# A hybrid two-layer backbone on one core: the last modulation chunks quarter by quarter, group 0 normed ahead, the pooling mean by a constant, the first mixer weights fetched sooner

## The chip, the core and the metric

The kernel runs on one core of a Trainium2 chip. The core has five engines that work side by side: TensorE (PE: matmuls; its weight loads are listed apart as PEld), VectorE (DVE), ScalarE (ACT), GpSimd (POOL) and SyncE (SP), which here only issues DMAs from HBM. The metric is the device time of one launch, in microseconds (us); lower is better. The time before is 3062.89 us, the median of 3 runs.

## What is computed

Two streams, latent `x` (256 tokens of width 2048) and context `ctx` (256 tokens), pass through two layers. Each layer has a token mixer and a gated MLP, both behind an RMS norm with a shift, a scale and a gate that come from the conditioning vectors through `w_mod`. Layer 0's mixer is a centred mean over 2, 4, 8 or 16 tokens (one window for each quarter of the channels) minus the token itself, then a 512x512 matrix for each channel group:

```python
POOL_WINDOWS = (2, 4, 8, 16)

def pool_mix(u, w, b, scale):
    for g, win in enumerate(POOL_WINDOWS):
        left, right = win // 2, win - 1 - win // 2
        ug = uf[..., g * POOL_GROUP:(g + 1) * POOL_GROUP]
        cs = jnp.cumsum(jnp.pad(ug, ((0, 0), (left + 1, right), (0, 0))), axis=1)
        window_sum = cs[:, win:win + T] - cs[:, :T]
        count = (jnp.minimum(t + right, T - 1) - jnp.maximum(t - left, 0) + 1).astype(jnp.float32)
        parts.append(window_sum / count[None, :, None] - ug)
    y = jnp.einsum('btgc,gcd->btgd', p, w).reshape(B, T, D) + b
    return y * scale

for i in range(DEPTH):                       # DEPTH = 2
    ml = (silu_c @ w_mod[i] + b_mod[i]).reshape(B, 6, 1, D)
    a_lat = modulate(rms_norm(h, norm1_g[i]), ml[:, 0], ml[:, 1])
    h = h + ml[:, 2] * mixer(a_lat)          # pool_mix in layer 0, attention in layer 1
    h = h + ml[:, 5] * conv_ffn(modulate(rms_norm(h, norm2_g[i]), ml[:, 3], ml[:, 4]), ...)
```

`count` is the window's width but for the first and last few tokens, where the window is cut off. The change concerns layer 0 alone: its modulation, its mixer and the start of its MLP.

## The kernel before

The hidden state is held transposed, as 16 tiles of 128 channels by 256 tokens for each stream (`hl`, `hc`). Every large product is made in float32 precision by three matmuls: weights and activations are split into a high part (`h`, made by ACT) and the rest (`l`, made by DVE) in a reduced type, and hi·hi, hi·lo and lo·hi are summed.

**Modulation.** Layer 0's modulation has 24 chunks of 512 outputs; chunk `4*w+g` belongs to use `w` (0 shift, 1 scale, 2 gate of the mixer; 3 to 5 the same of the MLP) and channel group `g`. `mod_pe` (L195) makes one chunk on PE: four quarters `g` of the contraction, each fetched as two DMAs of 512 KB into two tiles, in order. Two quarters are multiplied together: sixteen matmuls (L207), the first of which waits for the four DMAs of both. Then ACT copies the sum out of PSUM (`modev`, L219), PE transposes it (`modt`, L224) and DVE makes `modT` from it. The generator `mods` (L440) goes through the chunks in the order 0, 4, 8, 16, 12, then the same plus 1 and so on for each channel group, and 20 to 23 (the MLP's gate) last. `need(n)` (L453) advances it until n quarters have been issued.

**Rooms.** A fetched tile takes a staging room: six rooms of their own (`NW`), and such activation buffers (`A4` to `A15`) as are not yet in use, which `lend` adds and takes away by group and step (`LENT`, L41). `stage` (L115) hands the rooms out strictly in turn, so a DMA waits until the tile that was in its room half a ring or more before has been used. From step 13 of the last group on only the six rooms are left, three pairs.

**The mixer** (`mixer`, L461) is a generator too, one for each channel group: for its four channel tiles, DVE multiplies h by the scale and the norm's factor (`py`, L474), ACT adds the shift into a padded tile (`pad`, L476), DVE sums the window by doubling (`ws`, L482), POOL multiplies by a table of 1/count (`pf`, L487), DVE subtracts the token (L488) and splits (`ph`). After the fourth, the mixer's weights `wp` are loaded and split (L494). Then PE's `pm` (L505 to L507), ACT's `pz` with scale and bias, POOL's sum into the hidden state, and `Ad`, the split operand of the next products.

**The first MLP columns** (`partial`, L531) are made while the mixer works: for the first eight column tiles of the gate and up weights (`wcg`, `wcu`), the products of channel group g are made while group g+1 is mixed (`cg`, `cu`, L566 to L568, with the shift's share `pwg`, `pwu` from L549 transposed by `ptg`, `ptu`). Between them, `between(half)` (L606) calls `need`, the next step of the mixer, and in the last group the second norm, its operands (`normalise`, L373 ff.) and the gates of finished columns (`gate0`, `late`). When the last group is through, the dense stage starts with column 8 (`g`, L653). The numbers in `STEPS` (L459) say how many quarters must have been issued before each step of the first group's mixer.

**What sets the order.** The program is written in this order, but each engine's own order is then made by a scheduler from a model of the time; what an engine executes is shown by the rows further below. SP issues the DMAs in one queue, in its own order: a DMA that waits for its room holds up all behind it.

## Time and profile before

| | |
|---|---|
| median of 3 runs (lowest, highest) | 3062.89 us (3062.56, 3066.64) |
| the profiled execution's own time | 3060.9 us |
| its span in the trace | 3059.1 us |
| mean clock granted to PE | 0.989 |
| PE busy | 2977.4 us, 97% of the span |
| DVE, ACT, POOL busy | 1939.4, 1371.3, 829.1 us |
| HBM read | 554.93 MB |

The profile is of one execution. "Busy" is the time in which an engine had an instruction at work; a wait is put down to what ended last before the instruction could start. A row of a group reads: line, engine, operation, tile written <- tiles read, shape, count, then busy us and mean ns of one, then the engine's idle time just before and what ended it. A row of a window reads: stretch, length, then busy time and count for PE, PEld, DVE, ACT and POOL, the clock granted to PE (1.00 is full speed), the share of the DMA engines in use, and GB/s. A row of the chain of waits reads: start, duration, engine and what it did (DMA: from issue to landing).

### The profile page before, as it was taken

What the parts mean: (1) busy time and instruction counts of PE and PEld (TensorE: products, weight loads), DVE (VectorE), ACT (ScalarE), POOL (GpSimd) and SP (SyncE); (2) the same over time, 40 slices, a digit from 0 to 9 for tenths busy, and PEclk for the clock granted to TensorE, in tenths of its full rate; (3) what the DMA queues carried; (4) which work ended last, traced back from release to release, by engine and by line L of the source; (5) the groups of instructions that cost most, each with busy time, mean ns of one, the idle gap of its engine ahead of it and who ended that gap; (6) DMA issues with size and microseconds to landing.
All of it is one profiled execution on the core that took longest, in us unless ns stands there. A gap on an engine that the chain in (4) does not pass through costs nothing.

```text
span 3059.1 us, 40876 instructions
## 1 busy us (share of the span) xinstructions
PE 2977.4 (97%) x15082; PEld 2416.9 (79%) x15082; DVE 1939.4 (63%) x2748; ACT 1371.3 (45%) x2219; POOL 829.1 (27%) x823
## 2 busy tenths in 40 slices
PE   5999989999999999999999999999999999999998
PEld 2666668888888888888887888878888888888887
DVE  4455764386584857758586656474767666666666
ACT  3433455323333242433334444343545666666665
POOL 2111313303122030321312000000003566566665
PEclk9999989999999999999999999999999999999999
DMA  9888563384765747567482333333355555555563
GB/s 390 331 305 321 207 206 97 103 255 142 216 192 166 241 143 234 160 198 212 150 257 69 121 101 114 101 107 111 106 161 182 185 181 196 192 187 182 184 196 113
DMA packets 177927, 559.70 MB, mean 183 GB/s; under 512 B 17600, under 2 KB 22208, under 8 KB 177728
## 3 DMA queue, kind: packets, MB, share of 16 engines
q1 hardware_dynamic: 177728, 557.10, 55.7%
q8 instruction: 119, 1.95, 0.2%
q14 instruction: 80, 0.66, 0.1%
HBM read 554.93 MB, written 2.10 MB: 182 GB/s over the span
## 4 chain that ended last, share of the span: by engine, by line
PE 93%; DMA 2%; DVE 1%; POOL 1%; ACT 1%; issue 1%; SPq 0%; DVEq 0%; ACTq 0%; POOLq 0%
PE g L788 5%; PE u L788 5%; PE d L679 5%; PE d L680 5%; PE d L681 5%; PE d L835 4%; PE g L653 4%; PE g L655 4%; PE g L654 4%; PE u L655 4%; PE u L653 4%; PE u L654 4%; PE g L791 3%; PE u L791 3%; PE mod L207 2%; PE d L839 2%
## 5 line engine op out<-in xcount | busy, mean ns | idle before, releaser
L692 POOL TENSOR_TENSOR hl<-hl,dy 128x256 f32<-128x256 f32 x160 | 146.2, 914 | 941.8 <-ACT dy L691 941.6
L850 POOL TENSOR_TENSOR hl<-hl,dy 128x256 f32<-128x256 f32 x320 | 332.1, 1074 | 188.3 <-ACT dy L848 186.0
L262 DVE SCALAR_TENSOR_TENSOR macc<-wm,sc,macc 128x512 f32<-128x512 f32 (+1 forms) x360 | 328.8, 944 | 66.9 <-DMA wm<-wmod 66.2
L691 ACT ACTIVATE dy<-d,modT 128x256 f32<-128x256 f32 x320 | 133.1, 469 | 187.5 <-PE d L681 167.2
L692 POOL TENSOR_TENSOR hc<-hc,dy 128x256 f32<-128x256 f32 x160 | 129.4, 809 | 0.0
L848 ACT ACTIVATE dy<-d,modT 128x512 f32<-128x512 f32 x160 | 104.5, 684 | 43.0 <-PE d L839 41.5
L149 DVE TENSOR_TENSOR wd_2l<-wd,wd_2h 128x1024 fp32r<-128x1024 f32 (+1 forms) x44 | 54.5, 1245 | 107.8 <-ACT wd_2h L147 106.6
L207 PE MATMUL mod<-wm,sc 128*32 128x512 f32 x768 | 98.9, 641 | 15.2 <-DMA wm<-wmod 13.4
L937 POOL TENSOR_TENSOR rk<-rk,rp 128x256 f32<-128x256 f32 x16 | 13.2, 826 | 365.3 <-DVE rk L936 309.7
L149 DVE TENSOR_TENSOR wd_3l<-wd,wd_3h 128x1024 fp32r<-128x1024 f32 (+1 forms) x44 | 52.0, 1202 | 77.3 <-ACT wd_3h L147 75.9
L149 DVE TENSOR_TENSOR wd_1l<-wd,wd_1h 128x1024 fp32r<-128x1024 f32 (+1 forms) x44 | 53.7, 1224 | 54.4 <-ACT wd_1h L147 54.4
L487 POOL TENSOR_TENSOR pf<-ws,inv 128x256 f32<-128x256 f32 x32 | 29.3, 935 | 208.0 <-DVE ws L482 192.9
L149 DVE TENSOR_TENSOR wd_0l<-wd,wd_0h 128x1024 fp32r<-128x1024 f32 (+1 forms) x44 | 54.6, 1248 | 40.9 <-ACT wd_0h L147 40.9
L147 ACT CAST wd_1h<-wd 128x1024 fp32r<-128x1024 f32 (+1 forms) x44 | 45.3, 1032 | 74.8 <-PE u L654 49.4
L1026 ACT ACTIVATE sb<-sb,nm 128x512 f32<-128x512 f32 x64 | 46.1, 721 | 64.5 <-DVE nm L1022 63.3
L207 PEld LDWEIGHTS mod<-wm,sc 128*32 128x32 f32 x768 | 22.3, 114 | 65.5 <-issue 62.0
L147 ACT CAST wd_0h<-wd 128x1024 fp32r<-128x1024 f32 (+1 forms) x44 | 45.3, 1032 | 59.1 <-PE u L788 29.1
L814 DVE TENSOR_TENSOR actb<-sgb,actb 128x256 fp32r<-128x256 f32 x43 | 52.7, 1226 | 26.5 <-ACT actb L813 26.5
L679 PE MATMUL d<-act,wd_2h 128*128 128x512 f32 x172 | 67.1, 390 | 0.0
L681 PE MATMUL d<-act,wd_2l 128*128 128x512 f32 x172 | 66.9, 389 | 0.0
L680 PE MATMUL d<-act,wd_2h 128*128 128x512 f32 x172 | 66.9, 389 | 0.0
L679 PE MATMUL d<-act,wd_0h 128*128 128x512 f32 x172 | 66.9, 389 | 0.0
(1752 smaller groups left out, 9274.6 us busy)
## 6 DMA issues: line engine op xcount, KB each, us to landing
wm<-wmod SPq DMA_DIRECT2D x384, 512.0 KB, 6.1
wd<-wd SPq DMA_DIRECT2D x168, 512.0 KB, 4.4
wg<-wg SPq DMA_DIRECT2D x156, 512.0 KB, 4.7
wu<-wu SPq DMA_DIRECT2D x156, 512.0 KB, 4.5
wv<-wv SPq DMA_DIRECT2D x32, 512.0 KB, 3.7
wk<-wq SPq DMA_DIRECT2D x32, 512.0 KB, 4.0
wq<-wq SPq DMA_DIRECT2D x32, 512.0 KB, 3.6
wo<-wo SPq DMA_DIRECT2D x32, 512.0 KB, 4.2
```

The costliest lines, as they stand in the source:

```text
L149: eng.tensor_tensor(lo[:, :n], t[:, :n], hi[:, :n].bitcast(F32), op=ALU.subtract)
L262: nc.vector.scalar_tensor_tensor(acc[s], v, sc2[:, k, s : s + 1], acc[s], op0=ALU.mult, op1=ALU.add)
L653: nc.tensor.matmul(ps, hi[:, c : c + P], xh, start=(k == 0), stop=False)
L654: nc.tensor.matmul(ps, hi[:, c : c + P], xl, start=False, stop=False)
L655: nc.tensor.matmul(ps, lo[:, c : c + P], xh, start=False, stop=(k == KT - 1))
L679: nc.tensor.matmul(ps, hi[:, o : o + P], xh, start=(i == 0), stop=False)
L680: nc.tensor.matmul(ps, hi[:, o : o + P], xl, start=False, stop=False)
L681: nc.tensor.matmul(ps, lo[:, o : o + P], xh, start=False, stop=(i == n - 1))
L692: nc.gpsimd.tensor_tensor(h_of(s)[:, k, :], h_of(s)[:, k, :], y[:, s], op=ALU.add)
L788: nc.tensor.matmul(ps, hi[:, c : c + P], flat(B[k]), start=(k == 0), stop=False)
L791: nc.tensor.matmul(ps[:, T:], lo[:, c : c + P], B[k][:, 0], start=False, stop=(k == KT - 1))
L850: nc.gpsimd.tensor_tensor(hl[:, k, :], hl[:, k, :], y[:, q], op=ALU.add)
```

## The change

Five edits, all in layer 0:

1. `mod_pe`: for the chunks 21, 22 and 23 each quarter's eight matmuls go alone, behind its own two DMAs; the other chunks go in pairs of quarters as before.
2. Group 0's h times the norm's factor (eight 128x256 products on DVE, into two tiles `xn`) is made right after the norm, ahead of the modulation. When the scale and shift are there, one ACT instruction applies both and writes `pad`. Groups 1 to 3 keep `py`.
3. Pooling: the multiplication by 1/count on POOL is gone. DVE makes window sum times 1/win minus the token in one instruction. The first win/2 and the last win-1-win/2 columns of the window sum are multiplied beforehand, in place, by win/count: one tiny DVE instruction for each channel tile in group 0, two in the others.
4. `wp0` is loaded ahead of chunk 8's weights, and split where it was.
5. The last two steps of group 0's mixer ask for 15 quarters, not 17.

```diff
--- before.py
+++ after.py
@@ -195,25 +195,25 @@
     def mod_pe(l, ch, sc, pool):
 
         ps = bank("m", f"mod{l}_{ch}")
+        held = []
         for g in range(4):
             ts = load(lambda a, b: wmod[l, ch, g, :, a:b], 2048, f"wm{l}_{ch}_{g}")
-            if g % 2 == 0:
-                held, first = ts, fetched[-2:]
-            else:
-                landing = first + fetched[-2:]
+            held.append((g, ts, fetched[-2:]))
+            if ch > 20 or g % 2:
                 with ExitStack() as behind:
-                    for n, (gg, tt) in enumerate(((g, ts), (g - 1, held))):
+                    for n, (gg, tt, _) in enumerate(held[::-1]):
                         for j in (2, 3, 0, 1):
                             ins = nc.tensor.matmul(ps[32 * j : 32 * j + 32, :], sc[:, 4 * gg + j, :],
                                                    tt[j // 2][0][:, 512 * (j % 2) : 512 * (j % 2) + 512],
-                                                   start=(g == 1 and n == 0), stop=(g == 3 and n == 1),
-                                                   tile_position=(0, 32 * j))
+                                                   start=(g < 2 and (n == 0 and held[0][0] == 0)),
+                                                   stop=(g == 3 and gg == held[0][0]), tile_position=(0, 32 * j))
                             if n == 0 and j == 2:
-                                for x in landing:
+                                for x in sum((d for _, _, d in held), []):
                                     tc.add_manual_dep(ins.ins, x.name, mybir.DependencyInfo(
                                         mybir.DependencyClass.Sync, mybir.DependencyReason.DATA), reason="whole")
                                 behind.enter_context(tc.issue_after(ins.ins))
                                 behind.enter_context(tc.high_priority())
+                held = []
             if g == 3:
                 ev = pool.tile([P, 512], F32, tag="t2", name=f"modev{l}_{ch}")
                 nc.scalar.copy(ev, ps)
@@ -425,6 +425,11 @@
                 t = st.tile([P, 2, WP], F32, bufs=1, name=f"pad{j}")
                 nc.gpsimd.memset(t, 0.0)
                 pads.append(t)
+            normed = [act_tile(f"xn{j}", F32) for j in range(2)]
+            for k in range(4):
+                for s in both:
+                    nc.vector.tensor_tensor(normed[k // 2][:, k % 2, T * s : T * s + T], h_of(s)[:, k, :],
+                                            rs1[:, T * s : T * s + T], op=ALU.mult)
             shs = []
             for j in range(2):
                 t = st.tile([P, 4, 32], F32, bufs=1, name=f"sh{j}")
@@ -457,6 +462,7 @@
 
 
             STEPS = (9, 9, 9, 9, 13, 13, 17, 17)
+            STEPS0 = (9, 9, 9, 9, 13, 13, 15, 15)
 
             def mixer(g):
 
@@ -469,11 +475,16 @@
                 for i in range(4):
                     k = 4 * g + i
                     pad = pads[k % 2]
-                    y = f0.tile([P, 2, T], F32, tag="t2", name=f"py{k}")
+                    if g:
+                        y = f0.tile([P, 2, T], F32, tag="t2", name=f"py{k}")
+                    else:
+                        y = normed[k // 2][:, k % 2].rearrange("p (s t) -> p s t", s=2)
                     for s in both:
-                        nc.vector.scalar_tensor_tensor(y[:, s], h_of(s)[:, k, :], M(0, 1, k, s), rs1[:, T * s : T * s + T],
-                                                       op0=ALU.mult, op1=ALU.mult)
-                        nc.scalar.activation(pad[:, s, PAD : PAD + T], y[:, s], AF.Identity, bias=M(0, 0, k, s))
+                        if g:
+                            nc.vector.scalar_tensor_tensor(y[:, s], h_of(s)[:, k, :], M(0, 1, k, s),
+                                                           rs1[:, T * s : T * s + T], op0=ALU.mult, op1=ALU.mult)
+                        nc.scalar.activation(pad[:, s, PAD : PAD + T], y[:, s], AF.Identity, bias=M(0, 0, k, s),
+                                             scale=1.0 if g else M(0, 1, k, s))
                     src, w = pad, 1
                     while w < win:
                         n = WP - 2 * w + 1
@@ -482,16 +493,20 @@
                         nc.vector.tensor_tensor(dst[:, :, :n], src[:, :, :n], src[:, :, w : w + n], op=ALU.add)
                         src, w = dst, 2 * w
                     o = PAD - win // 2
+                    for c, n in ((0, win // 2), (T - (win - 1 - win // 2), win - 1 - win // 2)):
+                        if n:
+                            e = src[:, :, o + c : o + c + n]
+                            nc.vector.scalar_tensor_tensor(e, e, float(win), inv_t[:, c : c + n].unsqueeze(1).broadcast_to([P, 2, n]),
+                                                           op0=ALU.mult, op1=ALU.mult)
                     pf = f0.tile([P, 2, T], F32, tag="t2", name=f"pf{k}")
-                    for s in both:
-                        nc.gpsimd.tensor_tensor(pf[:, s, :], src[:, s, o : o + T], inv_t, op=ALU.mult)
-                    nc.vector.tensor_tensor(pf, pf, pad[:, :, PAD : PAD + T], op=ALU.subtract)
+                    nc.vector.scalar_tensor_tensor(pf, src[:, :, o : o + T], 1.0 / win, pad[:, :, PAD : PAD + T],
+                                                   op0=ALU.mult, op1=ALU.subtract)
                     ph = ap0.tile([P, 2, 2, T], F32R, tag=f"A{k}", name=f"ph{k}")
                     nc.scalar.copy(ph[:, 0], pf)
                     nc.vector.tensor_tensor(ph[:, 1], pf, ph[:, 0].bitcast(F32), op=ALU.subtract)
                     pa.append(ph)
                     if i == 3:
-                        parts = ld(wp[g], f"wp{g}")
+                        parts = split(early, "wp0") if g == 0 else ld(wp[g], f"wp{g}")
                     yield
                 nc.vector.tensor_tensor(gsc, modT[0, 8 + g].rearrange("p i s -> p (i s)"), V("ps")[:, 8 * g : 8 * g + 8],
                                         op=ALU.mult)
@@ -590,7 +605,9 @@
                         nc.vector.tensor_tensor(w_, w_, t_, op=ALU.add)
             lend(range(4, KT))
             mix = mixer(0)
-            for n in STEPS:
+            need(8)
+            early = load(lambda a, b: wp[0][:, a:b], 2048, "wp0")
+            for n in STEPS0:
                 need(n + 2)
                 next(mix)
             rstd = None
```

PE has as many instructions as before. DVE's list has 28 rows more, POOL's 16 fewer.

How the rows move, at three places. **The front, 20 to 82 us.** On SP (`wm_8_q_c` is half c of quarter q of chunk 8; DMAs are issued in the order of the rows), before:

```order
L131 DMA wm_8_0_0_294<-wmod 128x1024
L131 DMA wm_8_0_1024_296<-wmod 128x1024
L465 DMA inv_314<-inv 128x256
L131 DMA wm_8_2_1024_312<-wmod 128x1024
L131 DMA wm_8_2_0_310<-wmod 128x1024
L131 DMA wm_8_1_1024_300<-wmod 128x1024
L131 DMA wm_8_1_0_298<-wmod 128x1024
L131 DMA wm_8_3_1024_388<-wmod 128x1024
L131 DMA wm_8_3_0_386<-wmod 128x1024
L131 DMA wp_1024_376<-wp 128x1024
L131 DMA wp_0_374<-wp 128x1024
```

Now:

```order
L131 DMA wp_0_294<-wp 128x1024
L131 DMA wp_1024_296<-wp 128x1024
L471 DMA inv_328<-inv 128x256
L131 DMA wm_8_1_1024_314<-wmod 128x1024
L131 DMA wm_8_1_0_312<-wmod 128x1024
L131 DMA wm_8_0_1024_310<-wmod 128x1024
L131 DMA wm_8_0_0_308<-wmod 128x1024
L131 DMA wm_8_3_1024_382<-wmod 128x1024
L131 DMA wm_8_3_0_380<-wmod 128x1024
L131 DMA wm_8_2_1024_326<-wmod 128x1024
L131 DMA wm_8_2_0_324<-wmod 128x1024
```

Both halves of `wp` moved from behind chunk 8 to ahead of it, and all of chunk 8 moved back by two DMAs. On PE there, the end of chunk 12 and the first column matmuls, before:

```order
L207 MATMUL mod_12_542<-wm_12_0_1024_545,sc 32x512 x2
L207 MATMUL mod_12_542<-wm_12_0_0_543,sc 32x512 x2
L207 MATMUL mod_12_542<-wm_12_3_1024_619,sc 32x512 x2
L207 MATMUL mod_12_542<-wm_12_3_0_617,sc 32x512 x2
L207 MATMUL mod_12_542<-wm_12_2_1024_561,sc 32x512 x2
L207 MATMUL mod_12_542<-wm_12_2_0_559,sc 32x512 x2
L566 MATMUL cg_0_595<-Ad_563,wcg_0h_587 128x512
L566 MATMUL cg_1_610<-Ad_563,wcg_0h_587 128x512
```

Now:

```order
L206 MATMUL mod_12_536<-wm_12_0_1024_539,sc 32x512 x2
L206 MATMUL mod_12_536<-wm_12_0_0_537,sc 32x512 x2
L581 MATMUL cg_0_585<-Ad_541,wcg_0h_565 128x512
L581 MATMUL cg_1_604<-Ad_541,wcg_0h_565 128x512
L206 MATMUL mod_12_536<-wm_12_3_1024_613,sc 32x512 x2
L206 MATMUL mod_12_536<-wm_12_3_0_611,sc 32x512 x2
L206 MATMUL mod_12_536<-wm_12_2_1024_594,sc 32x512 x2
L206 MATMUL mod_12_536<-wm_12_2_0_592,sc 32x512 x2
```

The first two `cg` moved between the two halves of chunk 12. **The up weights of group 0** (`wcu`) on SP, before:

```order
L131 DMA wm_1_0_1024_651<-wmod 128x1024
L131 DMA wm_1_0_0_649<-wmod 128x1024
L131 DMA wcu_0_1024_718<-wu 128x2x512
L131 DMA wcu_0_0_716<-wu 128x2x512
L131 DMA wm_1_2_1024_700<-wmod 128x1024
L131 DMA wm_1_2_0_698<-wmod 128x1024
L131 DMA wm_5_1_1024_796<-wmod 128x1024
L131 DMA wm_5_1_0_794<-wmod 128x1024
```

Now:

```order
L131 DMA wm_5_0_1024_779<-wmod 128x1024
L131 DMA wm_5_0_0_777<-wmod 128x1024
L131 DMA wm_5_3_1024_827<-wmod 128x1024
L131 DMA wm_5_3_0_825<-wmod 128x1024
L131 DMA wm_5_2_1024_816<-wmod 128x1024
L131 DMA wm_5_2_0_814<-wmod 128x1024
L131 DMA wcu_0_0_710<-wu 128x2x512
L131 DMA wcu_0_1024_712<-wu 128x2x512
```

They moved twelve rows back, behind the last quarter of chunk 5. **The tail, 380 to 429 us.** On PE around chunk 22, before:

```order
L568 MATMUL cg_5_3254<-Ad_2819,wcg_4l_3185 128x512
L207 MATMUL mod_22_3234<-wm_22_1_1024_3263,sc 32x512 x2
L207 MATMUL mod_22_3234<-wm_22_1_0_3261,sc 32x512 x2
L207 MATMUL mod_22_3234<-wm_22_0_1024_3237,sc 32x512 x2
L207 MATMUL mod_22_3234<-wm_22_0_0_3235,sc 32x512 x2
L207 MATMUL mod_22_3234<-wm_22_3_1024_3330,sc 32x512 x2
L207 MATMUL mod_22_3234<-wm_22_3_0_3328,sc 32x512 x2
L207 MATMUL mod_22_3234<-wm_22_2_1024_3306,sc 32x512 x2
L207 MATMUL mod_22_3234<-wm_22_2_0_3304,sc 32x512 x2
L224 MATMUL modt_22_3364<-ident,modev_22_3340 128x128 x4
```

Now, around its last quarter:

```order
L583 MATMUL cg_5_3252<-Ad_2813,wcg_4l_3179 128x512
L206 MATMUL mod_22_3228<-wm_22_3_1024_3328,sc 32x512 x2
L206 MATMUL mod_22_3228<-wm_22_3_0_3326,sc 32x512 x2
L583 MATMUL cg_996<-Ad_2808,wcg_4l_3183 128x512
L581 MATMUL cg_996<-Ad_2813,wcg_4h_3182 128x512
L582 MATMUL cg_996<-Ad_2813,wcg_4h_3182 128x512
L583 MATMUL cg_996<-Ad_2813,wcg_4l_3183 128x512
L581 MATMUL cu_1197<-Ad_2784,wcu_4h_3405 128x512
L582 MATMUL cu_1197<-Ad_2784,wcu_4h_3405 128x512
L581 MATMUL cu_1268<-Ad_2784,wcu_4h_3405 128x512
L582 MATMUL cu_1268<-Ad_2784,wcu_4h_3405 128x512
L224 MATMUL modt_22_3358<-ident,modev_22_3334 128x128 x4
```

The quarters moved apart; matmuls of `cg` and `cu`, which do not need them, fill the places between and the one ahead of the transposes. On DVE at the tail's end, up to `late`, which the dense stage's first gate needs, before:

```order
L149 TENSOR_TENSOR wg_8l_3606<-wg_8_0_3601,wg_8h_3605 128x1024
L334 TENSOR_SCALAR A_0_3_3441<-nrm_3442,modT_14_2136,A_0_3_3441 128x256 x2
L579 TENSOR_TENSOR part_954<-part_954,cu_5_3472 128x512
L393 TENSOR_TENSOR sg_3459<-sg_3459,part_708 128x512
L400 TENSOR_TENSOR act_3462<-sg_3459,act_3462 128x512
L226 TENSOR_REDUCE modT_23_3521<-modt_23_3516 128x8
L189 TENSOR_TENSOR modT_23_3521<-modT_23_3521,vt 128x8
L589 TENSOR_REDUCE puu_4_3541<-ptu_4_3536 128x8
L376 TENSOR_TENSOR late_0_3551<-cg_960,n2acc 128x512
L376 TENSOR_TENSOR late_1_3555<-cu_1203,n2acc 128x512
```

Now:

```order
L149 TENSOR_TENSOR wg_8l_3600<-wg_8_0_3595,wg_8h_3599 128x1024
L400 TENSOR_TENSOR act_3456<-sg_3453,act_3456 128x512
L594 TENSOR_TENSOR part_948<-part_948,cu_5_3466 128x512
L149 TENSOR_TENSOR wu_8l_3661<-wu_8_0_3656,wu_8h_3660 128x1024
L149 TENSOR_TENSOR wg_8l_3604<-wg_8_1024_3597,wg_8h_3603 128x1024
L226 TENSOR_REDUCE modT_23_3515<-modt_23_3510 128x8
L189 TENSOR_TENSOR modT_23_3515<-modT_23_3515,vt 128x8
L604 TENSOR_REDUCE puu_4_3535<-ptu_4_3530 128x8
L376 TENSOR_TENSOR late_0_3545<-cg_954,n2acc 128x512
L376 TENSOR_TENSOR late_1_3549<-cu_1197,n2acc 128x512
```

Two more splits of the dense stage's weights (`wu_8l`, the second `wg_8l`) moved ahead of `late`.

## The prediction

> **What bounds the kernel now.** I read the page's first part, then the waits of TensorE (PE), then windows, then the chain of waits inside the stretches where PE is not full.
>
> ```profile
> span 3059.1 us, 40876 instructions
> PE 2977.4 (97%) x15082; PEld 2416.9 (79%) x15082; DVE 1939.4 (63%) x2748; ACT 1371.3 (45%) x2219; POOL 829.1 (27%) x823
> ```
>
> PE idles for 3059.1 − 2977.4 = 81.7 us in all. The change leaves PE's instructions as many as they were, so it can win only from this idle time and from matmuls that ran at a reduced clock, or lose by adding to them. Where the idle time lies before 450 us, by what ended it (total, times, longest):
>
> ```profile
> PE n1s L310 <- DVE n1q L303: 21.8, 1, 21.8
> PE mod L207 <- DMA wm<-wmod: 13.4, 3, 7.9
> PE modt L224 <- ACT modev L219: 11.1, 9, 3.3
> PE pwg L549 <- DVE sh L438: 3.4, 1, 3.4
> ```
>
> The 21.8 us at the start (square sums of the inputs) are not touched. The rest falls into two stretches, which the windows show (the columns from PE on are busy time and count; near the end the granted clock, DMA share and GB/s):
>
> ```profile
> 20.00:40.00 20.00, 15.08 (x86) 6.34 (x86) 3.03 (x11) 1.75 (x3) 1.03 (x1) 1.00 1.03 419
> 40.00:60.00 20.00, 12.09 (x50) 6.02 (x51) 16.35 (x29) 8.59 (x15) 6.70 (x8) 0.68 1.03 418
> 80.00:100.00 20.00, 20.00 (x125) 13.56 (x118) 5.74 (x13) 7.84 (x15) 0.00 (x0) 1.00 1.01 382
> 380.00:400.00 20.00, 12.96 (x68) 8.99 (x64) 15.25 (x29) 11.38 (x24) 3.51 (x3) 0.89 0.69 239
> 400.00:420.00 20.00, 17.37 (x87) 9.27 (x88) 11.05 (x20) 10.33 (x18) 1.74 (x1) 0.69 0.75 244
> ```
>
> In the **front** (20 to 80 us) the DMA share is 1.03: the queue is full, and an earlier transfer there only makes another later. In the **tail** (380 to 429 us) it is 0.69: there transfers wait for room, not for bandwidth. The chain of waits in the tail:
>
> ```profile
> 391.11 1.93 PE mod L207 x16
> 393.51 7.25 DMA wm<-wmod
> 403.27 4.84 DMA wm<-wmod
> 424.24 1.92 PE mod L207 x16
> 428.15 0.61 DVE late L376
> 428.80 0.50 PE g L653
> ```
>
> The first two quarters of chunk 22 leave their four rooms only when their sixteen matmuls have run (391.11 to 393.04). The last quarter is fetched into them at 393.51 and lands 7.25 us later; PE stands still. Then the same again for chunk 23: a transfer that starts at 403.27 and takes 4.84. The first matmul of the dense stage (g of column 8) comes at 428.80; from there PE has no large hole, so I count the time by how much earlier that matmul starts.
>
> **The singles in the tail.** A chunk above 20 now goes quarter by quarter: a quarter waits for two transfers instead of four and frees two rooms at once. On PE, quarters 0 to 3 of chunk 22 now stand apart between the column matmuls of group 3, where before its second sixteen stood behind all of them. What can be won is read from this row (the tail from chunk 21's end to the first dense matmul):
>
> ```profile
> 380.35:428.80 48.45, 37.17 (x197) 22.73 (x193) 31.22 (x59) 22.91 (x44) 6.58 (x5) 0.82 0.69 232
> ```
>
> PE is idle for 48.45 − 37.17 = 11.3 us of it. And what PE did right behind its holes was slow:
>
> ```profile
> 400.89 3.64 PE L207 MATMUL mod<-wm,sc 128*32 128x512 f32 x16 [7.93 <-DMA wm<-wmod]
> 408.24 3.64 PE L207 MATMUL mod<-wm,sc 128*32 128x512 f32 x16 [0.96 <-DMA wm<-wmod]
> ```
>
> Two sixteens ran in 3.64 us where the warm one at 424.24 took 1.92, which is 3.4 us more; the small work between them at the same clock (0.50) adds about 1.3. So PE alone could end 16.0 us earlier: the upper bound. VectorE (DVE) comes next: it is busy for 31.22 us, and its idle time is mostly this:
>
> ```profile
> DVE modT L226 <- PE modt L224: 13.2, 2, 10.4
> L149 DVE TENSOR_TENSOR wcg_4l<-wcg,wcg_4h 128x1024 fp32r<-128x1024 f32 x8 | 9.4, 1221 | 6.1 <-ACT wcg_4h L147 6.1
> ```
>
> The 13.2 us go away with PE's holes; the other idle time of DVE (48.45 − 31.22 − 13.2 = 4.0) I keep. By the new order two more splits of dense weights, 1.22 us each by the row of their kind, stand on DVE ahead of `late`, whose end PE awaits. So DVE ends at 380.35 + 31.22 + 4.0 + 2.4 = 418.0 where it ended at 428.8: **−10.8 us**. I take this rather than 16.0 since DVE is the longer of the two. The lower bound is the rooms: the last fourteen pairs of transfers still pass through six rooms, three pairs at a time. If only the longest hole (7.9) is halved and the clock recovers for one of the sixteens (1.7), the gain is 5.6.
>
> **The front.** `wp0` is fetched ahead of chunk 8, group 0 is normed ahead, and its scale and shift are one ScalarE (ACT) instruction.
>
> ```profile
> 40.26 10.78 DMA wp<-wp
> 51.06 1.99 ACT L147 CAST wp0h<-wp 128x1024 fp32r<-128x1024 f32 x2 [0.90 <-DMA wp<-wp]
> 54.90 1.12 PE L224 MATMUL modt<-ident,modev 128*128 128x128 f32 x4 [3.35 <-ACT modev L219]
> 56.02 0.43 PE pm L505
> 60.72 0.38 PE pm L507
> 61.33 0.23 PE pm L506
> 76.42 0.66 PE modt L224 x4
> 77.08 3.57 PE mod L207 x32
> 80.65 0.66 PE cg L566 x2
> ```
>
> `wp0` now lands where chunk 8's first half did, and the second half of chunk 8 lands at `wp0`'s old 51.04. So PE gets the last sixteen of chunk 8 at 51.04; with 1.92 for them and ACT's copy (0.6, no longer behind the 1.99 of `wp0h`) its transposes come near 54. Thus pm starts near 55, hardly sooner than now. What changes is the clock: PE works from 51 on, with no hole of 3.35 us ahead of the transposes, so pm's first dozen matmuls go at 0.23 instead of 0.43 (the spacing from 56.02 to 60.72): 12 × 0.20 = 2.4, of which I take 2.0. And of the 32 matmuls of chunk 12 (3.57 us, all between the transposes at 76.42 and the first column matmul at 80.65) the second sixteen now stand behind the first two column matmuls, which wait for chunk 16 and not for them: of their 1.8 us I take 1.1, since the column matmuls' own operands come in time for only part of it. Against it: `wcu` of group 0 now uses the rooms of `wcg` and is issued behind chunk 5, not at 78.
>
> ```profile
> 78.10 0.89 SPq L131 DMA_DIRECT2D wcu<-wu  x2
> 91.58 1.02 PE pwg L549 x16
> 97.05 0.43 PE cu L566
> DMA to landing us min/median/max: 4.2/6.7/9.0
> ```
>
> Its rooms come free with pwg, which starts at about 91.6 − 3.1 = 88.5 and takes 1.02; 4.2 to 6.7 us to land gives 93.7 to 96.3. PE wants it at 97.05 − 1.0 − 3.1 = 93.0: late by 0.7 to 3.3; cold work behind it is short, I take 1.1. Front: −2.0 − 1.1 + 1.1 = **−2.0 us**, with bounds of −4.4 (no stall, full 2.4, 2.0 for chunk 12's half) and +1 (nothing gained, `wcu` late).
>
> **The middle: pooling off GpSimd (POOL).**
>
> ```profile
> L487 POOL TENSOR_TENSOR pf<-ws,inv 128x256 f32<-128x256 f32 x32 | 29.3, 935 | 208.0 <-DVE ws L482 192.9
> L488 DVE TENSOR_TENSOR pf<-pf,pad 128x512 f32<-128x512 f32 x16 | 11.0, 687 | 7.0 <-POOL pf L487 7.0
> L474 DVE SCALAR_TENSOR_TENSOR py<-hc,modT,rs 128x256 f32<-128x256 f32 x16 | 11.6, 724 | 0.0
> L438 DVE COPY sh<-modT 128x8 f32<-128x8 f32 x4 | 0.7, 169 | 0.1
> ```
>
> POOL loses 32 × 0.935 = 29.3 us. DVE keeps sixteen 128x512 operations (one that multiplies and subtracts, about the 0.69 of the subtraction) and gets 28 tiny ones; by the nearest small row 0.17 each, 4.8 us, against the py of group 0 (8 × 0.72 = 5.8) that leave for idle time ahead of chunk 0 (3.03 us busy in 20 to 40). PE is 20.00 of 20 busy in 80 to 100 and nearly so through groups 1 to 3, so what DVE does there is hidden; its stall at pwg (3.4 us) hangs on `sh`, whose order is the same. I take +0.3, bounds −1 and +1.5. If that cover were gone, the 4.8 us would be the price.
>
> **Sum**, against the profiled execution (3060.9 us, 1.8 around its span of 3059.1): −10.8 − 2.0 + 0.3 = −12.5, 3048.4. The median of the runs shown, 3062.89, is 2.0 above the profiled execution, so 3050.4: I predict 3050.
>
> **Rivals.** *Everything comes back.* DVE's idle time shrinks as well and PE alone sets the tail: −16.0, front −4.4, middle −1: 3060.9 − 21.4 + 2.0 = 3041.5. For it: DVE has 4.0 us of idle left in my sum. Against it: DVE's 31.22 us of work do not shrink.
>
> *The rooms still bind.* There are three pairs, and a pair is free only when its split or its matmuls are done; the 7.9 us hole becomes a few of 2 to 3. Tail −5.6, front 0, middle +0.3: 3060.9 − 5.3 + 2.0 = 3057.6. For it: the chain above shows 4.84 and 7.25 from issue to landing, and a quarter's own matmuls last half of 1.92, so they cover little of it.
>
> *The tail stays cold; slower.* The singles stand in PE's order ahead of column matmuls that are ready, and each waits for its own two transfers: eight or more stops in place of three. This row shows what the clock did after the long hole:
>
> ```profile
> 396.00:406.00 10.00, 4.33 (x19) 1.37 (x20) 0.02 (x1) 1.30 (x2) 0.00 (x0) 0.50 0.53 176
> ```
>
> It was 0.50 all through, though PE worked for 4.33 us of it. If stops of this kind are spread over the whole tail, its 37.17 − 4.7 = 32.4 us of full-speed work go at the rate of the cold sixteens (3.64 to 1.92): 61.5 us, end at 441.9, +13.1; with the front 3060.9 + 13.1 − 2.0 + 0.3 + 2.0 = 3074.3. It is slower by over 0.2% once the tail ends after 436.5. Against it: the column matmuls between two singles are 1 to 5 us of work, and quarters 0 to 2 are fetched before PE asks for them. [...]
>
> **How the numbers follow.** Forecast 0.62; all comes back 0.12; rooms bind 0.17; cold tail 0.09. The range reaches from the first rival to a little past the second, 3041 to 3059, and leaves out the slower case and the ends of the others. About 0.2% (6.1 us) is what a measurement can tell: faster is below 3056.8, slower above 3069.0. The forecast and the first rival are faster, 0.74; of the rooms case 0.04 falls below 3056.8 and 0.13 between; slower is 0.09.
>
> **What would show it.** Tail: the wait of mod for wm in TensorE's waits falls from 13.4 to under 6, g of column 8 starts at 415 to 419, and DVE has no idle of 10 us. Front: pm from about 55 at 0.23 spacing, the first cg before 78, a wait of pwu or cu on `wcu` of 1 to 3 us. Middle: POOL down by 29 us, PE still full. I am wrong if g of column 8 starts later than 424, if the granted clock in the tail is 0.5 over more than 15 us, or if a new wait of more than 3 us stands in groups 1 to 3.

## The result, and the profile after

| | before | with the change |
|---|---|---|
| median (lowest, highest; runs) | 3064.14 us (3062.56, 3066.77; 8) | 3056.11 us (3052.68, 3057.03; 8) |
| the profiled execution, its span | 3060.9, 3059.1 us | 3052.68, 3050.9 us |
| PE, DVE, ACT, POOL busy | 2977.4, 1939.4, 1371.3, 829.1 us | 2971.1, 1930.7, 1371.8, 801.5 us |

The ratio is 0.9972, with a 95% interval of 0.9963 to 0.9982: 8 us faster. A second series of the same kernel gave 0.9976 (0.9966 to 0.9987). Forecast were 3050 and, between profiled executions, −12.5 us; measured between them is −8.2. The median of 3056.11 lies nearer to the 3057.6 of the rival "the rooms still bind" than to 3050. Both medians lie above their profiled execution by about 3.3 us, so the profiles can be compared.

The waits of TensorE before 450 us, with the change (total, times, longest):

```profile
PE n1s L310 <- DVE n1q L303: 21.7, 1, 21.7
PE mod L206 <- DMA wm<-wmod: 8.3, 4, 3.1
PE modt L224 <- ACT modev L219: 7.9, 5, 3.2
PE pwg L564 <- DVE sh L443: 3.4, 1, 3.4
PE g L670 <- DVE late L376: 2.3, 1, 2.3
PE cu L581 <- ACT wcu_4h L147: 1.9, 1, 1.9
PE pwu L564 <- DMA wcu<-wu: 1.6, 1, 1.6
PE cg L582 <- DVE Ad L539: 1.3, 1, 1.3
PE cg L581 <- ACT Ad L538: 1.3, 2, 0.8
```

The longest wait for a chunk's weights fell from 7.9 to 3.1 us. Of the 8.3 us of waiting for chunks that are left, 6.9 stand in the front (at 37, 45 and 50 us) and only 1.4 in the tail. In their place stand small waits that were not there or were shorter: `late` 2.3 instead of 0.9, `wcu_4h` 1.9, `wcu` 1.6, and `Ad` 2.6 instead of 0.7 (at 165, 249 and 335 us, in groups 1 to 3). The windows (columns as in the profile before):

```profile
40.00:60.00 20.00, 12.98 (x75) 5.91 (x75) 12.30 (x26) 10.12 (x19) 1.42 (x2) 0.83 1.03 418
60.00:80.00 20.00, 16.83 (x93) 8.86 (x90) 8.04 (x16) 11.73 (x24) 4.29 (x6) 0.91 1.03 410
80.00:100.00 20.00, 17.97 (x117) 10.66 (x115) 2.51 (x6) 4.93 (x7) 0.00 (x0) 1.00 0.99 369
380.00:400.00 20.00, 16.95 (x91) 10.30 (x91) 18.06 (x34) 13.28 (x26) 4.54 (x3) 1.00 0.84 300
400.00:420.00 20.00, 17.58 (x106) 10.83 (x106) 15.04 (x30) 11.55 (x20) 3.35 (x2) 1.00 0.83 291
```

In the tail PE is busy 34.5 of 40 us where it was 30.3, all of it at clock 1.00 (0.89 and 0.69 before). In 80 to 100 us it now idles 2.0 us; it was full there before. Since a change in one place can be lost in the next, I followed fixed points of the program through both profiles: `pwg` and `pwu` of group 0, then the second `pwg` (start, duration, instruction, idle time ahead and its cause). Before:

```profile
91.51 1.09 PE L549 MATMUL pwg<-wcg,sh 128*32 128x256 f32 x16
95.96 1.09 PE L549 MATMUL pwu<-wcu,sh 128*32 128x256 f32 x16
116.86 1.08 PE L549 MATMUL pwg<-wcg,sh 128*32 128x256 f32 x16
```

With the change:

```profile
89.00 1.09 PE L564 MATMUL pwg<-wcg,sh 128*32 128x256 f32 x16
97.15 0.59 PE L564 MATMUL pwu<-wcu,sh 128*32 128x256 f32 x2 [1.63 <-DMA wcu<-wu]
116.93 1.08 PE L564 MATMUL pwg<-wcg,sh 128*32 128x256 f32 x16
```

The front is 2.5 us ahead at the first point, 1.2 behind at the second (1.9 us of chunk matmuls now stand ahead of it that came later before), and level at the third. Nothing of it reaches the rest: the same `pwg` of the last group starts at 352.07 before and 351.94 with the change. The gain is made after that: the first dense matmul starts at 419.68, not 428.80, 9.1 us sooner.

The 9.1 us hold until 2300 us. Then 0.9 of them is lost, between 2305 and 2340 us, at the seam between layer 1's mixer and its MLP, which the change does not touch. This is chance. From layer 1's `modt_0s` matmuls (637.42 with the change) to the end, the fourteen profiles of this case take 2410.6 to 2415.4 us, and no edit reaches there. A difference of 1 or 2 us between two spans therefore says little, and the experiments below are read at fixed points ahead of 640 us.

The end of the tail with the change, on PE:

```profile
416.26 0.66 PE L224 MATMUL modt<-ident,modev 128*128 128x128 f32 x4
416.76 0.60 PE L597 MATMUL ptu<-ident,peu 128*128 128x128 f32 x4
419.68 0.50 PE L670 MATMUL g<-A,wg_8h 128*128 128x512 f32 x1 [2.32 <-DVE late L376]
```

and on DVE:

```profile
412.61 1.23 DVE L149 TENSOR_TENSOR wg_8l<-wg,wg_8h 128x1024 fp32r<-128x1024 f32 x1 [4.20 <-ACT wg_8h L147]
415.76 1.72 DVE L149 TENSOR_TENSOR wu_8l<-wu,wu_8h 128x1024 fp32r<-128x1024 f32 x1 [0.73 <-ACT wu_8h L147]
417.41 1.21 DVE L149 TENSOR_TENSOR wg_8l<-wg,wg_8h 128x1024 fp32r<-128x1024 f32 x1
418.94 0.68 DVE L376 TENSOR_TENSOR late<-cg,n2acc 128x512 f32<-128x512 f32 x1
```

The last transposes come 10.6 us sooner than before (426.82), but the dense matmul behind them waits 2.3 us: `late` stands on DVE behind two splits that start only at 415.76, when their data is there. DVE is not short of time here: it idles 4.20 us just before 412.61 and 0.73 just before 415.76. Ahead of the 4.20, ACT's cast to `wg_8h` itself waits 3.99 us for the DMA of `wg`.

### The profile page after: what moved, and what is told of

Its sections match the earlier page's. It is cut to its first block, busy times and chain, and to the rows that moved or that the text cites. A ratio compares the mean times of both kernels' runs of the same rounds, so it can differ in the third digit from the quotient of the medians.

```text
span 3050.9 us, 40895 instructions
## 1 busy us (share of the span) xinstructions
PE 2971.1 (97%) x15082; PEld 2412.8 (79%) x15082; DVE 1930.7 (63%) x2776; ACT 1371.8 (45%) x2219; POOL 801.5 (26%) x791
## 4 chain that ended last, share of the span: by engine, by line
PE 87%; DVE 1%; POOL 1%; DMA 1%; issue 1%; ACT 1%; SPq 0%; DVEq 0%; POOLq 0%; ACTq 0%
PE g L805 5%; PE u L805 5%; PE d L696 5%; PE d L697 5%; PE d L698 5%; PE d L852 4%; PE g L670 4%; PE g L672 4%; PE g L671 4%; PE u L670 4%; PE u L671 4%; PE u L672 4%; PE u L808 3%; PE g L808 3%; PE d L856 2%; PE k L980 2%
## 5 line engine op out<-in xcount | busy, mean ns | idle before, releaser
L262 DVE SCALAR_TENSOR_TENSOR macc<-wm,sc,macc 128x512 f32<-128x512 f32 (+1 forms) x360 | 328.8, 944 | 69.0 <-DMA wm<-wmod 68.4
L529 POOL TENSOR_TENSOR hl<-hl,pz 128x256 f32<-128x256 f32 x16 | 14.9, 933 | 280.9 <-ACT pz L527 202.6
L696 PE MATMUL d<-act,wd_0h 128*128 128x512 f32 x172 | 66.9, 389 | 0.0
L697 PE MATMUL d<-act,wd_0h 128*128 128x512 f32 x172 | 66.9, 389 | 0.0
```

What stands on the lines that cost most here:

```text
L262: nc.vector.scalar_tensor_tensor(acc[s], v, sc2[:, k, s : s + 1], acc[s], op0=ALU.mult, op1=ALU.add)
L696: nc.tensor.matmul(ps, hi[:, o : o + P], xh, start=(i == 0), stop=False)
L697: nc.tensor.matmul(ps, hi[:, o : o + P], xl, start=False, stop=False)
```

## The experiments

A ratio is to the kernel before, run on the same chip in turns, with its 95% interval; 0.001 is 3.1 us. Each program has also one profile. Where a program's profile is its slowest execution, this is said; those of the change, `late_first` and `best16` are their fastest.

**1. The first edit alone** (`singles_only`): the hunk in `mod_pe` of the change, nothing else. Its main line:

```diff
+            if ch > 20 or g % 2:
```

> The kernel before with the first edit alone (chunks 21 to 23 quarter by quarter). Theory (the tail's singles bring everything): the first dense matmul (g of column 8), 428.8 us before and 419.7 with the whole change, starts at 419 to 421; ratio to before 0.9970 to 0.9975, that is 8 to 9 us. Rival (the singles need VectorE relieved of the slower pooling work to pay): first dense matmul at 423 or later, 5 us or less.

Ratio 0.9979 (0.9970 to 0.9989), 3055.98 us. The first dense matmul starts at 421.38 in a profile whose front was 0.9 us behind; from the last group's `pwg` (352.94) to it, it takes 68.4 us, against 76.7 before and 67.7 with the whole change. So the first edit alone makes 8.3 of the tail's 9.0 us. The predicted ratio was 0.9970 to 0.9975; the interval holds it, the value is 1 us short, and the dense matmul is 0.4 us later than the 419 to 421 that I gave. The rival falls: it asked for 423 or later, so no relief of VectorE is needed for the tail. The 0.7 us between the two tails need not come from the other edits either: from 352 to 358 us the granted clock is 0.51 here, as before, and 0.72 with the whole change.

**2. The change without the first edit** (`no_singles`). The hunk in `mod_pe` is undone; its first lines:

```diff
-            held.append((g, ts, fetched[-2:]))
-            if ch > 20 or g % 2:
+            if g % 2 == 0:
+                held, first = ts, fetched[-2:]
+            else:
+                landing = first + fetched[-2:]
...
```

> The whole change without the first edit: all chunks again in pairs of quarters; the norm ahead, the pooling on VectorE, the early wp and the 15 quarters stay. Theory: the front's gain is gone by 117 us, so the first dense matmul is at 428 to 429.5 and the time within 1.5 us of before; TensorE's wait of mod for wm in the tail stays near 8 us. Rival (front and pooling pay 2 to 3 us that the profile of the whole change hides): 2 to 3 us faster.

Ratio 0.9992 (0.9983 to 1.0001), 3060.57 us: 2 us less, not told from no change. By its size this is the rival's time; the theory had at most 1.5 us. The first dense matmul is at 428.10, where the theory had it, and the long wait is back (waits of PE from 380 to 432 us):

```profile
PE mod L207 <- DMA wm<-wmod: 8.9, 2, 7.9
PE g L670 <- DVE late L376: 0.9, 1, 0.9
```

For the tail this settles it: without the first edit the gain there is gone. Whether the other four edits bring 2 us elsewhere, this ratio cannot tell.

**3. Pooling without GpSimd, alone** (`pool_only`).

```diff
+                    for c, n in ((0, win // 2), (T - (win - 1 - win // 2), win - 1 - win // 2)):
+                        if n:
+                            e = src[:, :, o + c : o + c + n]
+                            nc.vector.scalar_tensor_tensor(e, e, float(win), inv_t[:, c : c + n].unsqueeze(1).broadcast_to([P, 2, n]),
+                                                           op0=ALU.mult, op1=ALU.mult)
...
-                    for s in both:
-                        nc.gpsimd.tensor_tensor(pf[:, s, :], src[:, s, o : o + T], inv_t, op=ALU.mult)
-                    nc.vector.tensor_tensor(pf, pf, pad[:, :, PAD : PAD + T], op=ALU.subtract)
+                    nc.vector.scalar_tensor_tensor(pf, src[:, :, o : o + T], 1.0 / win, pad[:, :, PAD : PAD + T],
+                                                   op0=ALU.mult, op1=ALU.subtract)
```

> The kernel before with the third edit alone (pooling without GpSimd, the ends corrected by 28 tiny VectorE instructions). Theory: GpSimd 28 us less busy, TensorE as full as before in groups 1 to 3, time within 1.5 us of before. [...]

Ratio 0.9994 (0.9985 to 1.0003), 3061.18 us, first dense matmul at 429.13: no change that can be told, as the theory had it. VectorE does gain: its `py` rows of 128x256 take 0.48 us each, where they took 0.72 and 0.60 beside the GpSimd products, and in spite of 28 more rows it is not busier (1932.7 us for 1939.4). By itself this wins no time that can be measured. This was not the last word (experiment 9).

**4. Sixteen quarters instead of fifteen** (`steps16`, and once more as `steps16_again`), on the whole change. The up weights of group 0 then take rooms that come free earlier, and are issued before chunk 1's last quarters.

```diff
-            STEPS0 = (9, 9, 9, 9, 13, 13, 15, 15)
+            STEPS0 = (9, 9, 9, 9, 13, 13, 16, 16)
```

> The whole change, with 16 in place of 15 in the last two steps of group 0's mixer, so that group 0's up weights take the rooms of chunk 12's second quarter, not those of wcg, and are issued some 20 us sooner. Theory (the late up weights lose what the front gained): no wait for wcu near 97 us, the second pwg at 115 (116.9 before and with the change), 1.5 to 2.5 us faster than the whole change, ratio to before 0.9963 to 0.9968. Rival (in the front the full transfer queue is the bound): another transfer is then late, the second pwg stays at 116.5 to 117, ratio as with the whole change, 0.9972.

Ratio 0.9962 (0.9950 to 0.9975), 3050.91 us, a little beyond the theory's 0.9963 to 0.9968. But the profile had the second `pwg` at 116.86, as the rival said. It was the slowest of five executions (3056.3; the others 3046 to 3053), with the clock at half speed from 44 to 61 us (0.50 in the windows of 2 us from 44 to 60, 0.78 from 60 to 62). So the same program was run again:

> steps16 once more, for a second profile: the first was taken in its slowest execution (3056.3, the others 3046 to 3053). Theory (the first profile had the front at half clock from 44 to 61 us, and that alone cost its gain): this profile has the clock back by 54 us, the second pwg at 112 to 114, first dense matmul at 416.5 to 418.5. Rival (16 quarters bring nothing in the front, the shorter times come from elsewhere): second pwg at 116.5 or later also with a full clock.

Again 0.9962 (0.9950 to 0.9975), 3050.32 us, and now the profile agrees. The window from 40 to 60 us, first profile:

```profile
40.00:60.00 20.00, 11.58 (x47) 4.85 (x48) 11.89 (x25) 8.56 (x15) 0.00 (x0) 0.60 1.03 418
```

second profile:

```profile
40.00:60.00 20.00, 13.17 (x75) 6.19 (x75) 11.90 (x26) 9.64 (x19) 1.42 (x2) 0.83 1.02 418
```

and its fixed points:

```profile
86.19 1.09 PE L564 MATMUL pwg<-wcg,sh 128*32 128x256 f32 x16
90.63 1.09 PE L564 MATMUL pwu<-wcu,sh 128*32 128x256 f32 x16
111.64 1.09 PE L564 MATMUL pwg<-wcg,sh 128*32 128x256 f32 x16
```

With a granted clock of 0.83, as in the profile of the whole change, `pwu` has no wait and the second `pwg` is 5.3 us earlier. Of these, some 0.9 us is work that now stands behind it; at the last group's `pwg`, which has the same work ahead of it in both, 5.1 us are still there (346.86). The first dense matmul came at 415.27, sooner than expected (416.5 to 418.5). The rival falls. The first profile shows what a long half-clock stretch costs, some 17 us in place of 7: with the same program, 5.2 us at the second `pwg` and 5.2 at the last group's (352.06).

**5. The change once more** (`after_again`), no edit.

> The whole change once more, for a second profile of the same program. Theory (what the front gains is lost at the late up weights in every execution): a wait of pwu for wcu of 1 to 2 us near 97 us, second pwg between 116 and 118 as before, first dense matmul at 419 to 421; median 3054 to 3057. Rival (the loss at 97 us was one execution's luck): no such wait, second pwg at 114 or earlier.

3055.54 us; the wait of `pwu` for `wcu` is there again (1.61 us, at 97.06), the second `pwg` is at 118.37, the first dense matmul at 420.62. The second `pwg` is 0.4 us outside the expected 116 to 118; the loss is no luck of one execution. All four profiles of programs with 15 have this wait (1.12 to 1.69 us), none of the seven with 16 or 17.

**6. Seventeen quarters** (`steps17`): the fifth edit undone.

```diff
-            STEPS0 = (9, 9, 9, 9, 13, 13, 15, 15)
+            STEPS0 = (9, 9, 9, 9, 13, 13, 17, 17)
```

> The whole change without its fifth edit: the last two steps of group 0's mixer ask for 17 quarters again. Theory (it is the 15 that puts group 0's up weights into the rooms of wcg): no wait for wcu near 97 us, 1.5 to 3 us faster than the whole change, ratio to before 0.9962 to 0.9967. Rival (the 15 helps since wcg comes sooner): first column matmul 1 to 2 us later than with the whole change, ratio 0.9972 or above.

Ratio 0.9966 (0.9952 to 0.9979), 3050.05 us; no wait for `wcu`, `pwu` at 91.55, second `pwg` at 112.39, 4.5 us sooner than with the change and with the same work ahead of it. So far the theory holds, though the ratio's interval overlaps with that of the change. In this profile the gain does not last: the last group's `pwg` is at 350.78, and the first dense matmul at 419.85, no sooner than with the change. At 246.13 `cg` waits 1.60 us for `Ad` (0.44 with the change), and behind it PE is at half clock:

```profile
247.50:251.00 3.50, 3.50 (x10) 2.71 (x9) 1.91 (x5) 1.45 (x4) 0.00 (x0) 0.51 1.00 378
```

From 350 to 357 us it is at 0.52 once more. That this execution is still 2.7 us shorter than the change's comes from behind 637 us, where the programs do not differ. What the fifth edit costs is read better from pairs of profiles with the same clock (experiments 4 and 8).

**7. `late` ahead of the two splits** (`late_first`), on the whole change: DVE's part of the splits of `wu_8` and of the second half of `wg_8` is bound behind `late`.

```diff
...
+                for first, ins in hold_lo:
+                    if j >= first:
+                        behind.enter_context(tc.issue_after(ins))
                 eng.tensor_tensor(lo[:, :n], t[:, :n], hi[:, :n].bitcast(F32), op=ALU.subtract)
...
-                    nc.vector.tensor_tensor(r, HELD[f, q], late_norm[0], op=ALU.mult)
+                    behind_late[:] = [nc.vector.tensor_tensor(r, HELD[f, q], late_norm[0], op=ALU.mult).ins]
...
+                hold_lo[:] = [(nm == "g", ins) for ins in behind_late] if f == NS else []
                 parts = ld(wsrc[0, f], f"w{nm}0_{f}")
+                hold_lo[:] = []
```

> The whole change, with VectorE's splits of the second half of wg of column 8 and of both halves of wu of column 8 bound behind the last late product. Theory (late stands behind two splits that wait for their transfers, 2.3 us): the first dense matmul waits for late less than 1 us and starts some 2 us sooner than with the whole change as counted from the last modulation transposes (3.4 us from these to the first dense matmul with the whole change, 1.0 to 1.5 now); 1.5 to 2 us faster than the whole change, ratio to before 0.9966. Rival (VectorE's work is the bound, only its order changes): the splits are late instead and the dense stage stops a few us on, nothing gained.

Ratio 0.9969 (0.9958 to 0.9981), 3052.55 us. PE at the tail's end:

```profile
415.04 0.60 PE L228 MATMUL modt<-ident,modev 128*128 128x128 f32 x4
416.95 0.50 PE L677 MATMUL g<-A,wg_8h 128*128 128x512 f32 x1 [0.88 <-DVE late L380]
```

DVE there:

```profile
415.68 0.19 DVE L230 TENSOR_REDUCE modT<-modt 128x8 f32<-128x32 f32 x1 [1.73 <-PE modt L228]
416.22 0.68 DVE L380 TENSOR_TENSOR late<-cg,n2acc 128x512 f32<-128x512 f32 x1
419.07 1.22 DVE L153 TENSOR_TENSOR wg_8l<-wg,wg_8h 128x1024 fp32r<-128x1024 f32 x1
420.21 2.35 DVE L153 TENSOR_TENSOR wu_8l<-wu,wu_8h 128x1024 fp32r<-128x1024 f32 x2
```

The wait for `late` is 0.88, and from the last transposes to the dense matmul it takes 1.9 us in place of 3.4: 1.5 won (I had put the 1.9 at 1.0 to 1.5). The splits that now come later are missed by nobody: from the first dense matmul to layer 1's `modt_0s` matmuls at 634.69 it takes 217.74 us, as with the whole change (419.68 to 637.42). DVE even waits 1.73 us for PE. So the rival, DVE's work as the bound, falls. The ratio alone would not tell 0.9969 from 0.9972.

**8. Both repairs** (`best16`): the edits of 4 and 7.

> late_first with 16 in place of 15 quarters as in steps16. Theory (both losses are real and lie in different stages): they add, 4 to 5 us faster than the whole change, ratio to before 0.9955 to 0.9960. Rival (one of them hides the other): no faster than steps16, 0.9962.

Ratio 0.9959 (0.9946 to 0.9971), 3048.20 us. The ratios cannot tell the theory from the rival, which asked for 0.9962. The profile has the first dense matmul at 415.11, 13.7 us sooner than before and 4.6 sooner than with the change; but experiment 4's second profile had it at 415.27 without the edit of 7. In that profile the wait for `late` is 2.42 us (here 0.88), and behind it the clock is 0.51 from 416.3 to 419.8 us, here 1.00. So I compare at `modt_0s`: 637.42 with the change, 634.61 with the edit of 4, 634.69 with that of 7, 632.85 with both. In these profiles the two win 2.8 and 2.7 us, together 4.6: they add but for 1.0.

`late_first` and `best16` differ in the fifth edit alone, and in both the granted clock is 0.74 over 40 to 60 us. The last group's `pwg` starts at 351.31 in the first and 347.67 in the second. This pair puts the cost of the 15 quarters at 3.6 us.

**9. `best16` with pooling on GpSimd again** (`best16_gpsimd`): experiment 3 turned round.

> best16 with the third edit undone: GpSimd multiplies by the table of 1/count again. Theory (pooling off GpSimd is worth nothing, the work lay beside TensorE's): same as best16 within 1.5 us, 3047 to 3050. Rival (with the front's other losses gone the pooling chain of group 0 now counts, since GpSimd's two products and the slower VectorE stand in the chain to pm): pm starts 1 us or more later than in best16 and 2 to 4 us are lost.

Ratio 0.9967 (0.9956 to 0.9978), 3052.48 us. The intervals overlap, but the profiles show where a difference of some 2.5 us can come from. ACT in `best16`, last of the pooling splits and the copy of chunk 8:

```profile
51.87 0.62 ACT L510 CAST ph<-pf 128x512 fp32r<-128x512 f32 x1 [1.41 <-DVE pf L507]
53.45 0.58 ACT L223 COPY modev<-mod 128x512 f32<-128x512 f32 x1 [0.96 <-PE mod L210]
```

and with GpSimd:

```profile
54.86 0.62 ACT L506 CAST ph<-pf 128x512 fp32r<-128x512 f32 x1 [0.60 <-DVE pf L504]
55.39 0.58 ACT L223 COPY modev<-mod 128x512 f32<-128x512 f32 x1
```

In the first, the copy waits for PE's matmuls of chunk 8; in the second, those were done by 52, and the copy stands on ACT behind the pooling splits, which are 3.0 us later. PE waits 4.02 us for the copy, and pm starts at 56.78, not 54.50. So the theory falls in this pair of profiles: with `wp0` early, pooling on GpSimd is the longer chain in the front, and the third edit pays 2.3 us at pm. The rest of that profile's difference (it ends 6 us later at 421.23) holds more than this chain; PE is at half clock just behind the start of pm (0.50 from 56 to 60 us), among other things.

**10. Idle matmuls in the front** (`fill16`), on `steps16`: five matmuls without use keep PE at work in its waits.

```diff
+FILL = {(4, 1): 1, (4, 4): 2, (8, 1): 2}
...
+    def fill(n, ins):
+        if not idle:
+            idle.append(bank("gu", "idle"))
+        with tc.issue_after(ins), tc.high_priority():
+            for _ in range(n):
+                nc.tensor.matmul(idle[0], ident, flat(hl[:, 0:2, :]), start=True, stop=True)
...
+            if l == 0 and (ch, g) in FILL:
+                fill(FILL[ch, g], ins.ins)
...
```

> steps16 with five idle matmuls (ident by two tiles of h, 128x512, about 0.85 us each, result unused) in TensorE's waits of 33 to 51 us: one behind the first half of chunk 4, two behind its transposes, two behind the first half of chunk 8. [...] Rival (the front is set by transfers and VectorE): pm starts no sooner, time as steps16 or up to 2 us slower since the idle matmuls delay the real ones.

Ratio 0.9975 (0.9966 to 0.9983), 3054.63 us; runs from 3050.59 to 3058.09. By the ratios that is some 4 us slower than `steps16`, with overlapping intervals; the rival allowed 2. The profile is the slowest execution. I had hoped for 1 to 3 us less than `steps16` from a full clock in the front: the clock was full up to 70 us, the gain did not come. Windows of this profile:

```profile
40.00:60.00 20.00, 14.71 (x76) 8.24 (x77) 11.89 (x26) 10.11 (x19) 1.43 (x2) 1.00 1.03 418
60.00:80.00 20.00, 17.52 (x94) 9.62 (x93) 8.06 (x17) 10.69 (x23) 4.27 (x6) 0.91 1.02 404
```

The clock is full from 40 to 60 us, and pm starts at 53.73, as in the change (53.66): the last sixteen matmuls of chunk 8 ahead of it still wait 1.78 us for their transfer, with the DMA share at 1.03. Then PE waits 2.48 us for a chunk's copy at 71.34 and is at half clock there (0.50 from 72 to 74 us). The runs lie 7.5 us apart, between the 10.0 and the 4.1 of the two series of `steps16`. The scheduler also ordered other rows anew, so what the later loss came from is not settled.

**11. Chunk 20 quarter by quarter as well** (`best16_20`), on `best16`.

```diff
-            if ch > 20 or g % 2:
+            if ch > 19 or g % 2:
```

> best16 with chunk 20 too quarter by quarter. Theory (singles pay where six rooms are left, and chunk 20 lies where more are lent): within 1.5 us of best16. Rival (singles pay wherever TensorE waits for a chunk): 1.5 us or more faster, less waiting of mod for wm between 340 and 380 us.

Ratio 0.9951 (0.9938 to 0.9965), 3046.42 us, the lowest of all, 1.8 us below `best16`, with overlapping intervals. Its profile is its slowest execution (3052.3) and shows a cold front (PE's clock at 0.62 from 40 to 60 us) and a wait of 4.67 us for a chunk's copy in the tail, so it cannot say where they come from. Neither theory is settled.

## Why the prediction was right, point by point

**The place and the sign of the tail** were right, and so was its mechanism. The hole of 7.9 us is gone, the long waits are at most 3.1, the tail's clock is 1.00, and experiment 1 gets 8.3 of the 9.0 us from the first edit alone. I gave the tail −10.8; it brought −9.0. Two of the signs that I set did not come: the waits for chunks fell to 8.3 us, not under 6, since 6.9 of them stand in the front, and the first dense matmul starts at 419.68, not between 415 and 419.

**The step that mis-sized it** is "the other idle time of DVE" of 4.0 us that I kept. The tail with the change, from the same start:

```profile
380.35:419.68 39.33, 34.21 (x192) 20.82 (x193) 32.43 (x63) 24.55 (x45) 7.55 (x5) 1.00 0.83 296
```

DVE is busy 32.4 us, 1.2 less than the 33.6 of my sum, and idle 39.33 − 32.43 = 6.9 us. Of these, 4.2 are one wait for `wg_8h`, whose weights are in transit. So the tail's end came 1.7 us behind the 418.0 of that sum, and not because DVE was full. That DVE "is the longer of the two" was right only in that `late` is queued behind splits that wait. What costs is the place of the two splits in DVE's order and the arrival of their data. Experiment 7 moves them and wins 1.5 us at that point without losing them later. Had DVE's work been the bound, it could have won nothing.

**The front** was sized at −2.0 and came to +0.1 at the second `pwg`. pm did start sooner (53.66; I had said about 55) and at full clock, but that is a matter of the execution: in the change's second profile it starts at 56.16. `wcu` was late by 1.63 and 0.39, inside the 0.7 to 3.3 that I gave; I took 1.1 from that range, and it came to 2.0. A second price of the 15 I did not see. ACT with the change:

```profile
69.12 1.99 ACT L147 CAST wcg_0h<-wcg 128x1024 fp32r<-128x1024 f32 x2 [1.07 <-DMA wcg<-wg]
71.33 0.56 ACT L219 COPY modev<-mod 128x512 f32<-128x512 f32 x1
```

and with 16 (experiment 4, second profile):

```profile
65.21 1.99 ACT L147 CAST wcg_0h<-wcg 128x1024 fp32r<-128x1024 f32 x2
69.58 0.57 ACT L219 COPY modev<-mod 128x512 f32<-128x512 f32 x1
```

With 15, SP issues `wcg` 4.4 us later (57.93 for 53.52), and its splits stand right ahead of the copy of chunk 16. PE waits 3.17 us for that copy (1.99 in each of the other three profiles with 15), and 1.44 with 16. So the gain was there to be had, and the change's own fifth edit gave it back: 5.1 us at the last group's `pwg` by experiment 4, of which some is the clock, and 3.6 by the pair in experiment 8. I priced it at 1.1 only.

**The middle** (+0.3) held within its bounds: from the second to the last group's `pwg` the change is 0.2 us quicker. The 4.8 us that I counted as more work for DVE did not show: over the whole run it is busy 1930.7 us for 1939.4, in part by the shorter `py` rows (experiment 3). That pooling is worth nothing held for the kernel before (experiment 3), and not for a kernel without the front's other waits (experiment 9).

**The rivals.** That everything comes back did not happen; it asked for the first dense matmul at 407.4 (428.8 − 21.4), and even `best16` has it at 415.11. The rooms do not bind much: one wait of 1.4 us for a chunk is left in the tail with the change. That the time came close to this rival's 3057.6 is luck for it, since the loss lies in the front and at the end of DVE's queue. The cold tail did not come: the clock is 1.00 in both windows of the tail. It is not sure to stay so: in `best16_20` the tail's last transposes took 1.11 us, not the 0.66 of the change (at 414.47 and 416.26), and in the second profile of `steps16` the clock is 0.51 from 416.3 to 419.8 us, just behind the first dense matmul.

The forecast of the profiled time was thus 4.3 us too low: 1.8 from the tail, 2.1 from the front, −0.5 from the middle, and 0.9 by chance from the seam in layer 1.

## What to carry to other kernels

When a staging ring runs short of rooms, let each consumer take the smallest piece that it can use: here the longest wait for a chunk fell from 7.9 to 3.1 us, with column matmuls in the gaps. Behind such a repair look at once at in-order queues: a split that waits for its transfer must not stand ahead of the operation that the next stage needs, as it did on DVE ahead of `late` (PE waited 2.32 us) and on ACT ahead of chunk 16's copy (3.17 us). And when a step count is lowered to start something sooner, look in the issue order at which buffers everything behind it now takes. And compare gains of a few us at fixed points of profiles whose clock agrees; one profile can show the wrong sign (experiment 4: the second `pwg` at 116.86 and at 111.64 with the same program).

## What the runs showed of the hardware

The front's clock is a matter of the execution, not only of the program: two profiles of `steps16` had 0.60 and 0.83 over 40 to 60 us, and its runs lay between 3046.3 and 3056.3 us. In windows of 2 us the clock is 0.50 from 44 to 50 and from 56 to 60 us before, and from 44 to 48 us with the change. With the change, PE's rows around the drop in the front are

```profile
37.36 1.92 PE L206 MATMUL mod<-wm,sc 128*32 128x512 f32 x16 [2.35 <-DMA wm<-wmod]
41.41 0.65 PE L224 MATMUL modt<-ident,modev 128*128 128x128 f32 x4 [2.13 <-ACT modev L219]
45.21 3.64 PE L206 MATMUL mod<-wm,sc 128*32 128x512 f32 x16 [3.15 <-DMA wm<-wmod]
```

and the windows

```profile
41.00:42.00 1.00, 0.59 (x4) 0.42 (x4) 1.00 (x1) 0.35 (x1) 0.00 (x0) 1.00 1.05 430
42.00:43.00 1.00, 0.06 (x1) 0.00 (x0) 0.62 (x4) 0.21 (x1) 0.00 (x0) 0.71 1.00 410
43.00:44.00 1.00, 0.00 (x0) 0.00 (x0) 0.09 (x1) 1.00 (x3) 0.00 (x0) 0.50 1.04 426
```

The clock fell within 42 to 43, less than 1 us after the transposes had ended at 42.06, with a hole of 2.13 us and 0.65 us of work before. The longest hole in these rows ahead of the drop is 2.35 us; what sets the moment of the drop, no run here shows. With the idle matmuls of experiment 10 the clock stayed at 1.00 through this stretch (40 to 60 us).
